# A gated-norm stage with its norm sums three products behind, its side sums dealt over the next group, and the next product's first weights made ahead

## The chip, the cores and the metric

The kernel runs on one core of a Trainium2 chip. The metric is the device time of one execution in microseconds. An execution is one launch of the whole program. The engines are named as in the profile: PE is TensorE (matmuls), PEld its weight loads, DVE VectorE, ACT ScalarE, POOL GpSimd, and SP SyncE, which here only issues DMAs.

## The reference

The program is one inference step of a small decoder trunk: a Mamba-2 (SSD) layer, then a sliding-window attention layer, each with an MLP. The part that the change touches is the end of the SSD mixer: the gate, a norm over each of eight groups of 256 features, and the output projection.

```python
def gated_group_rmsnorm(y, z, w):
    g = (y * jax.nn.silu(z)).astype(jnp.float32)
    shp = g.shape
    g = g.reshape(shp[:-1] + (N_GROUPS, shp[-1] // N_GROUPS))
    g = g * lax.rsqrt(jnp.mean(g * g, axis=-1, keepdims=True) + EPS)
    return (g.reshape(shp) * w.astype(jnp.float32)).astype(y.dtype)

# in mamba_mixer: z is the first D_INNER columns of rmsnorm(h) @ w_in, y the scan's output
    out = gated_group_rmsnorm(y, z, gate_w) @ w_out
```

D_MODEL is 1024, D_INNER 2048, N_GROUPS 8; there are 1104 columns (tokens): 1024 of the new sequence, 64 of the samples and 16 meta tokens.

## The kernel before

Activations lie with features on the 128 partitions and tokens along the free axis; one tile row covers 1104 tokens. Matmuls in fp32 are made of three products of a high and a low part (`mm3`): high weights by high data, high by low, low by high (L204, L205, L206). So everything that goes into a matmul is first split: ACT casts the high part, DVE or POOL subtracts it for the low part.

**The gates.** `gates_out` runs over the eight groups g. A group has two tiles of 128 features (j = 0, 1) and three blocks of columns c (384, 384 and 336, the table `CH`), so six gate products of 24 matmuls each. For each product ACT takes the tanh (L762) and DVE makes (t + 1) * z (L763). When both products of a block are done, POOL multiplies them by y (L770), which SP loads from DRAM (L754), ACT squares (L771), DVE adds the two squares (L772), and ACT and DVE split that sum of squares into its high part (`msh`, L247) and low part (`msl`, L248). The sum over the features is then two matmuls with a matrix of ones, L259 on the high part and L262 on the low part.

**When the sum comes.** The sum is not issued at once. `gate_group` puts it on the list `due` with a count, and `tick`, called after each product, counts down and issues what has reached 0. With the count 2 a block's sum comes two products later. What is issued is `gate_norm`: the two matmuls, then ACT copies the result to SBUF (L795). After the third block of a group it goes on at once: Ln and Exp on ACT (L798, L799), each of which loads its table, two scalings on DVE (L802, 128 x 1104 each, one for each j), and for the groups 0 to 5 the side sums.

**The side sums.** The output projection uses a scheme with seven products in place of eight on blocks of a two-by-two split; `side_sums` makes its sums of data. It takes the four halves r[0] to r[3] of the scaled tiles (two tiles, each in two halves of 552 columns), writes three of them and four sums of them to the DRAM buffer z_d (L818), and uses the norm's own tile gm for two of the sums (m and u). The last sum, r[2] - u, is made in two halves of 276 columns in small tiles o5 and written from there (L832). Groups 6 and 7 write their scaled tiles to DRAM (g_d) instead.

**Buffers.** y lives in two tiles that the groups take in turn, so group g + 2 is loaded into the tile of group g. The o5 tiles come from a ring of five (n1) which the high and low parts of the sums share; the n3 tiles of the products, from a ring of two. The sums have one PSUM bank.

**The output product.** `block_products` comes right behind the gates. `down_weights` is a generator that loads two tiles of weights and yields seven weight parts, some of them sums of weights on DVE (L1166, L1172), each split by ACT (L1047) and POOL (L1048). Its data come back from z_d (L1224) and are split by ACT and DVE (L1229, L1230). Its first outputs are added by DVE at L1264. At its sixth weight part `more` issues what is still on `due`, in a PSUM bank of the output product.

**What sets the order.** The code is written in one order, but a scheduler decides in what order each engine gets its instructions, from its own estimate of when each is ready. Within one engine the queue runs in order. Sums of groups above 0 are kept in program order on PE (`pin`).

## Time and profile before

| | us |
|---|---|
| three runs, median (lowest to highest) | 2924.53 (2918.5 to 2924.64) |
| the profiled execution | 2923.57 |
| its span in the profile | 2921.9 |
| gates, from the start of group 0's last norm sum to group 7's middle norm sum | 672.40 to 862.28 |
| first quarter of the output product's first block | 862.28 to 890.24 |
| DVE busy, whole span | 1895.0 |
| ACT busy, whole span | 1413.9 |
| POOL busy, whole span | 1386.1 |

In the rows of the profile the first number is a start or a stretch in us from the start of the span, "gm<-ms" reads output from input, and square brackets hold how long the engine had been idle before the instruction, and which instruction on another engine let it go. In a window's row each engine has its busy time and, in brackets, its number of instructions; the granted clock of PE, the DMA share and the rate in GB/s stand at the end.

### The profile page before, as it was taken

What the parts mean: (1) busy time and instruction counts of PE and PEld (TensorE: products, weight loads), DVE (VectorE), ACT (ScalarE), POOL (GpSimd) and SP (SyncE); (2) the same over time, 40 slices, a digit from 0 to 9 for tenths busy, and PEclk for the clock granted to TensorE, in tenths of its full rate; (3) what the DMA queues carried; (4) which work ended last, traced back from release to release, by engine and by line L of the source; (5) the groups of instructions that cost most, each with busy time, mean ns of one, the idle gap of its engine ahead of it and who ended that gap; (6) DMA issues with size and microseconds to landing.
All of it is one profiled execution on the core that took longest, in us unless ns stands there. A gap on an engine that the chain in (4) does not pass through costs nothing.

```text
span 2921.9 us, 51729 instructions
## 1 busy us (share of the span) xinstructions
PE 2816.2 (96%) x19895; PEld 2711.0 (93%) x19895; DVE 1895.0 (65%) x2995; ACT 1413.9 (48%) x2742; POOL 1386.1 (47%) x1279
## 2 busy tenths in 40 slices
PE   8999999988989999999999999999999999999998
PEld 6999999978889999999999999988889999999998
DVE  6788777765657675455466765666678454356675
ACT  6555555544555264444343325655555444433333
POOL 5566666665546615444266573312112444345562
PEclk9999999999999999999999999999999999999998
DMA  3344544447655224444554422447453444533422
GB/s 137 91 128 124 125 128 123 123 123 258 218 206 171 80 85 149 136 156 139 224 212 171 161 89 94 160 153 261 164 187 133 150 140 150 206 138 124 151 96 73
DMA packets 219470, 433.43 MB, mean 148 GB/s; under 512 B 30728, under 2 KB 128392, under 8 KB 216648
## 3 DMA queue, kind: packets, MB, share of 16 engines
q1 hardware_dynamic: 219224, 430.14, 44.3%
q8 instruction: 156, 2.56, 0.4%
q14 instruction: 90, 0.74, 0.1%
HBM read 302.71 MB, written 128.32 MB: 148 GB/s over the span
## 4 chain that ended last, share of the span: by engine, by line
PE 77%; DVE 10%; ACT 4%; issue 3%; DMA 3%; POOL 3%; SPq 0%; DVEq 0%; ACTq 0%; POOLq 0%
PE g L204 10%; PE g L206 10%; PE g L205 10%; PE mc L204 4%; PE mc L206 3%; PE mc L205 3%; PE ma L204 3%; PE ma L205 3%; PE ma L206 3%; PE md L206 3%; PE md L205 3%; PE md L204 3%; PE mb L206 3%; PE mb L204 3%; PE mb L205 3%
## 5 line engine op out<-in xcount | busy, mean ns | idle before, releaser
L1048 POOL TENSOR_TENSOR w<-s,w 128x384 fp32r<-128x384 f32 (+1 forms) x272 | 370.4, 1368 | 386.9 <-ACT w L1047 354.4
L206 PE MATMUL g<-S,w 128*128 128x384 f32 (+2 forms) x1584 | 531.1, 336 | 3.9 <-POOL w L171 3.3
L204 PE MATMUL g<-S,w 128*128 128x384 f32 (+2 forms) x1584 | 533.4, 337 | 1.3 <-DVE qp L1462 0.6
L205 PE MATMUL g<-S,w 128*128 128x384 f32 (+2 forms) x1584 | 533.6, 337 | 0.0
L1048 POOL TENSOR_TENSOR w<-raw,w 128x384 fp32r<-128x384 f32 (+1 forms) x204 | 264.3, 1301 | 286.2 <-ACT w L1047 255.2
L171 POOL TENSOR_TENSOR w<-raw,w 128x1024 fp32r<-128x1024 f32 x96 | 247.1, 2574 | 253.3 <-ACT w L170 189.3
L206 PEld LDWEIGHTS g<-S,w 128*128 128x128 f32 x1584 | 301.9, 191 | 5.8 <-POOL w L171 3.6
L204 PEld LDWEIGHTS g<-S,w 128*128 128x128 f32 x1584 | 301.3, 190 | 4.7 <-issue 1.5
L205 PEld LDWEIGHTS g<-S,w 128*128 128x128 f32 x1584 | 301.7, 190 | 0.9 <-issue 0.3
L1047 ACT CAST w<-s 128x384 fp32r<-128x384 f32 (+1 forms) x272 | 149.8, 557 | 313.0 <-DVE s L1172 84.7
L204 PE MATMUL ma<-S,w 128*128 128x276 f32 (+1 forms) x808 | 235.2, 291 | 8.0 <-DVE us L1264 6.7
L206 PE MATMUL ma<-S,w 128*128 128x276 f32 (+1 forms) x808 | 234.7, 290 | 0.0
L205 PE MATMUL ma<-S,w 128*128 128x276 f32 (+1 forms) x808 | 234.3, 290 | 0.0
L1047 ACT CAST w<-raw 128x384 fp32r<-128x384 f32 (+1 forms) x204 | 111.8, 555 | 154.6 <-PE mc L206 45.2
L602 DVE SCALAR_TENSOR_TENSOR fm<-xp,cv,fm 128x1024 f32<-128x1024 f32 x96 | 162.8, 1698 | 33.1 <-ACT fm L583 32.5
L204 PEld LDWEIGHTS ma<-S,w 128*128 128x128 f32 x808 | 153.3, 190 | 9.3 <-ACT S L1229 2.7
L205 PE MATMUL g<-R,w 128*128 128x384 f32 (+2 forms) x480 | 158.6, 330 | 0.0
L204 PE MATMUL g<-R,w 128*128 128x384 f32 (+2 forms) x480 | 158.1, 329 | 0.0
L206 PE MATMUL g<-R,w 128*128 128x384 f32 (+2 forms) x480 | 158.1, 329 | 0.0
L205 PEld LDWEIGHTS ma<-S,w 128*128 128x128 f32 x808 | 153.5, 190 | 0.0
L206 PEld LDWEIGHTS ma<-S,w 128*128 128x128 f32 x808 | 153.2, 190 | 0.0
L170 ACT CAST w<-raw 128x1024 fp32r<-128x1024 f32 x96 | 100.5, 1047 | 105.8 <-DMA raw<-in_w_o_dram 19.9
(492 smaller groups left out, 8696.0 us busy)
## 6 DMA issues: line engine op xcount, KB each, us to landing
raw<-in_w_up_dram SPq DMA_DIRECT2D x64, 512.0 KB
raw<-in_w_in_dram SPq DMA_DIRECT2D x48, 512.0 KB
raw<-in_w_downs_dram SPq DMA_DIRECT2D x64, 384.0 KB
w<-ws_o SPq DMA_DIRECT2D x48, 512.0 KB
w<-ws_q SPq DMA_DIRECT2D x40, 512.0 KB
ab<-acs_d SPq DMA_DIRECT2D x64, 256.0 KB
S<-t_d SPq DMA_DIRECT2D x18, 828.0 KB
S<-t_e SPq DMA_DIRECT2D x18, 816.0 KB
```

The lines of the kernel that those rows point to most:

```text
L170: nc.scalar.copy(out=wh, in_=raw)
L171: nc.gpsimd.tensor_tensor(out=wl, in0=raw, in1=wh.bitcast(F32), op=ALU.subtract)
L204: mm(out=out, lhsT=wh, rhs=xh, start=(first and k == 0), stop=False)
L205: mm(out=out, lhsT=wh, rhs=xl, start=False, stop=False)
L206: mm(out=out, lhsT=wl, rhs=xh, start=False, stop=(k == n - 1))
L602: nc.vector.scalar_tensor_tensor(out=acc[:, :SEQ], in0=xp[:, k:k + SEQ], scalar=cv[:, j, k:k + 1], in1=acc[:, :SEQ], op0=ALU.mult, op1=ALU ...
L1047: nc.scalar.copy(out=t[:, 0], in_=src)
L1048: nc.gpsimd.tensor_tensor(out=t[:, 1], in0=src, in1=t[:, 0].bitcast(F32), op=ALU.subtract)
```

## The change

The count in `due` goes from 2 to 3, so each norm sum comes three products behind its block. The work behind the third sum is no longer one piece: the first tile is scaled at once; the second scaling and the first part of the side sums are put at the head of `due` with the count 1, the rest with the count 2. For that `side_sums` becomes a generator with one yield; its other caller runs it through with `list`. With `own` it makes the last side sum as one operation of 552 columns in r[0], that is in the tile of y itself, and writes it from there. For the last group, at the fourth of its six steps, the generator of the output product's first weights is started and two of its parts are made; after the gates one pending sum (group 7's middle block) is issued in a bank of the output product, four more parts are made, and `block_products` takes these first.

```diff
--- before.py
+++ after.py
@@ -1,5 +1,6 @@
 from contextlib import ExitStack
 from functools import partial
+from itertools import chain
 
 import concourse.bass as bass
 import concourse.tile as tile
@@ -772,10 +773,10 @@
             nc.vector.tensor_tensor(out=g2[:, 0], in0=g2[:, 0], in1=g2[:, 1], op=ALU.add)
             self.tick()
             parts = self.sum_parts(g2[:, 0], n)
-            self.due.append([2, partial(self.gate_norm, g, c, y, parts, tmp)])
+            self.due.append([3, partial(self.gate_norm, g, c, y, parts, tmp)])
             if g == 0 and c < 2:
 
-                self.tick(2)
+                self.tick(3)
             yield
 
     def tick(self, n=1):
@@ -797,18 +798,24 @@
             return
         nc.scalar.activation(out=rs, in_=rs, func=AF.Ln, bias=self.eps4, scale=D / 256)
         nc.scalar.activation(out=rs, in_=rs, func=AF.Exp, scale=-0.5)
-        for j in range(2):
+
+        def scale(j):
             ft = 2 * g + j
             nc.vector.scalar_tensor_tensor(out=y[j], in0=y[j], scalar=self.nv[:, ft % 8, 6 + ft // 8:7 + ft // 8],
                                            in1=rs, op0=ALU.mult, op1=ALU.mult)
+        scale(0)
         if g < 2 * KB:
-            self.side_sums([t[:, i * T // 2:(i + 1) * T // 2] for t in y for i in range(2)],
-                           self.rz[g // KB][:, :, :, g % KB], rs[:, :T // 2], rs[:, T // 2:])
+
+            sums = self.side_sums([t[:, i * T // 2:(i + 1) * T // 2] for t in y for i in range(2)],
+                                  self.rz[g // KB][:, :, :, g % KB], rs[:, :T // 2], rs[:, T // 2:], True)
+            self.due[:0] = [[1, lambda: (scale(1), next(sums))], [2, lambda: list(sums)]]
         else:
+            scale(1)
             for j in range(2):
                 nc.sync.dma_start(out=self.gd[g][:, j], in_=y[j])
 
-    def side_sums(self, r, d, m, u):
+    def side_sums(self, r, d, m, u, own=False):
+
 
         nc = self.nc
         n = r[0].shape[1]
@@ -823,8 +830,14 @@
         to(0, 1, m)
         sub(r[1], r[3], r[1])
         to(1, 0, r[1])
+        yield
         sub(u, r[3], m)
         to(1, 1, u)
+        if own:
+
+            sub(r[0], r[2], u)
+            to(2, 1, r[0])
+            return
         for k in range(2):
             t = self.n1("o5")[:, :qw]
             cs = slice(k * qw, k * qw + qw)
@@ -854,8 +867,10 @@
         slots = [[[(t[:, 0], t[:, 1])] for t in ts] for ts in ([A5] + B + S[:4], [S[4], A5, A5] + S[:4])]
         load, parts = self.side_io(self.rz, slots)
         for g in range(1, G):
-            for _ in gate if g == 1 else self.gate_of(g, xs, yps):
-                pass
+            for k, _ in enumerate(gate if g == 1 else self.gate_of(g, xs, yps)):
+                if (g, k) == (G - 1, 3):
+                    gen = self.down_weights(self.i["w_outs"][0], 0)
+                    ahead = gen, [next(gen) for _ in range(2)]
             if g < G - 1:
                 self.split_ahead()
             if g == 4:
@@ -870,16 +885,19 @@
         cb.close()
         us = self.pool("us", ctx=co).tile([P, 4, nn], F32, name="us")
 
+        def free_bank_sums(n):
+
+            self.pstat = (self.pq, self.CHAIN[0][3], 1, 1024)
+            self.tick(n)
+            self.pstat = None
+
         def more(b, p, i):
             if (b, p) != (0, 0):
                 return
             if 1 <= i <= 4:
                 parts(0, i + 2)
             if i == 5:
-
-                self.pstat = (self.pq, self.CHAIN[0][3], 1, 1024)
-                self.tick(9)
-                self.pstat = None
+                free_bank_sums(9)
             if i == 6:
 
                 t = ya.tile([P, 4, nn], F32R, tag="y", bufs=1, name="A6")
@@ -887,8 +905,10 @@
                 slots[1][1] = [(rest, t[:, 0:2]), (t[:, 2:3], t[:, 3:4])]
         self.pq = self.pool("pq", space=PSUM, ctx=co)
         rd = [self.gd.get(g) for g in range(G)]
+        free_bank_sums(1)
+        ahead[1].extend(next(ahead[0]) for _ in range(4))
         self.block_products(self.i["w_outs"], big, us, slots, load, parts, [(0, 3, 4, 5, 6)], [(3, 6, 7, 8, 10)],
-                            (lambda: self.block_load(rd, 3, R0), lambda j: self.block_parts(j, R0)), more, (1, 1))
+                            (lambda: self.block_load(rd, 3, R0), lambda j: self.block_parts(j, R0)), more, (1, 1), ahead)
 
     def out_last(self, hts, done, norm):
 
@@ -1112,7 +1132,7 @@
         if not 2 <= f < 14:
             nc.sync.dma_start(out=rd[f].rearrange("p f (i n) -> p (f i) n", i=2), in_=r)
             return
-        self.side_sums([r[:, e] for e in range(4)], rt[(f - 2) // KB][:, :, :, (f - 2) % KB], m1, u)
+        list(self.side_sums([r[:, e] for e in range(4)], rt[(f - 2) // KB][:, :, :, (f - 2) % KB], m1, u))
 
     def up(self, layer, rd, rt, R0):
 
@@ -1230,7 +1250,9 @@
                 nc.vector.tensor_tensor(out=lo, in0=lo.bitcast(F32), in1=hi.bitcast(F32), op=ALU.subtract)
         return load, parts
 
-    def block_products(self, w, big, us, slots, load, parts, free, make, last, more, early=(0, 0)):
+    def block_products(self, w, big, us, slots, load, parts, free, make, last, more, early=(0, 0),
+                       ahead=None):
+
 
 
         nc = self.nc
@@ -1267,7 +1289,10 @@
                 banks = {}
                 hv = [[h[j][i][:, p] for i in range(2)] for j in range(2)]
                 uv = us[:, p]
-                for i, (wh, wl) in enumerate(self.down_weights(w[b], p)):
+                weights = self.down_weights(w[b], p)
+                if (b, p) == (0, 0) and ahead:
+                    weights = chain(ahead[1], ahead[0])
+                for i, (wh, wl) in enumerate(weights):
                     e = self.CHAIN[p % 2][i]
                     new = e not in banks
                     if new:
```

The line numbers of the changed kernel are higher by one to twenty-two: L802 is L804 there, L817 is L824, L818 is L825, L763 and L772 are L764 and L773, L248 is L249, L795 is L796, L754 is L755, L1166 is L1186, L1230 is L1250. Tiles carry a running number, which differs between the two.

On DVE, at the change from group 4 to group 5, before (gy_8540 is group 4's y, gm_8702 its norm, msl_8891 the low part of group 5's first sum):

```order
L802 SCALAR_TENSOR_TENSOR gy_8540<-gy_8540,nv_71,gm_8702 128x1104 x2
L763 SCALAR_TENSOR_TENSOR n3_8894<-n3_8894,g_8895 128x384
L817 TENSOR_TENSOR gm_8702<-gy_8540 128x552
L763 SCALAR_TENSOR_TENSOR n3_8894<-n3_8894,g_8922 128x384
L817 TENSOR_TENSOR gy_8540<-gy_8540 128x552
L817 TENSOR_TENSOR gm_8702<-gy_8540,gm_8702 128x552
L817 TENSOR_TENSOR o5_8884<-gy_8540,gm_8702 128x276
L817 TENSOR_TENSOR o5_8887<-gy_8540,gm_8702 128x276
L772 TENSOR_TENSOR n3_8894<-n3_8894 128x384
L248 TENSOR_TENSOR msl_8891<-n3_8807,msh_8890 128x384
```

The same place in the changed kernel (gy_8524 is group 4's y, gm_8718 its norm, msl_8852 and msl_8931 the low parts of group 5's first and middle sum):

```order
L773 TENSOR_TENSOR n3_8855<-n3_8855 128x384
L249 TENSOR_TENSOR msl_8852<-n3_8787,msh_8851 128x384
L804 SCALAR_TENSOR_TENSOR gy_8524<-gy_8524,nv_71,gm_8718 128x1104 x2
L249 TENSOR_TENSOR msl_8931<-n3_8855,msh_8930 128x384
L764 SCALAR_TENSOR_TENSOR n3_8934<-n3_8934,g_8935 128x336
L824 TENSOR_TENSOR gm_8718<-gy_8524 128x552
L764 SCALAR_TENSOR_TENSOR n3_8934<-n3_8934,g_8971 128x336
L824 TENSOR_TENSOR gy_8524<-gy_8524 128x552
L824 TENSOR_TENSOR gm_8718<-gy_8524,gm_8718 128x552
L824 TENSOR_TENSOR gy_8524<-gy_8524,gm_8718 128x552
```

The low part of group 5's first sum moved from behind all of group 4's scalings and side sums to ahead of both scalings; the scalings still stand together.

On ACT, around the copy of group 4's third sum, before (gy_8792 is group 5's y):

```order
L795 COPY gm_8702<-ms_8771 128x384
L170 CAST w_9046<-raw_9044 128x1024
L762 ACTIVATE n3_8807<-g_8835 128x384
L795 COPY gm_8702<-ms_8867 128x336
L798 ACT_TABLE_LOAD
L798 ACTIVATE gm_8702<-gm_8702,eps_67 128x1104
L771 ACTIVATE n3_8807<-gy_8792 128x384
```

and in the changed kernel (gy_8772 is group 5's y):

```order
L796 COPY gm_8718<-ms_8815 128x384
L772 ACTIVATE n3_8787<-gy_8772 128x384
L763 ACTIVATE n3_8855<-g_8890 128x384
L772 ACTIVATE n3_8855<-gy_8772 128x384
L772 ACTIVATE n3_8787<-gy_8772 128x384
L796 COPY gm_8718<-ms_8883 128x336
L799 ACT_TABLE_LOAD
```

The copy that starts group 4's norm, which stood between a product's tanh and its Ln, now has three squares of group 5 between it and the copy of the middle block.

On DVE, at the start of the output product, before (n3_9454 and msl_9519 belong to group 7's last block, S_90 is data of the output product, the s tiles are sums of weights):

```order
L772 TENSOR_TENSOR n3_9454<-n3_9454 128x336
L1230 TENSOR_TENSOR S_90<-S_90 128x1656
L248 TENSOR_TENSOR msl_9519<-n3_9454,msh_9518 128x336
L1166 TENSOR_TENSOR s_9564<-raw_9539 128x384
L1166 TENSOR_TENSOR s_9591<-raw_9537,raw_9539 128x384
```

and in the changed kernel, right behind group 6's two scalings (n3_9351 and msl_9422 belong to group 7's middle block, n3_9437 and msl_9503 to its last, hh is the output product's result):

```order
L773 TENSOR_TENSOR n3_9351<-n3_9351 128x384
L764 SCALAR_TENSOR_TENSOR n3_9437<-n3_9437,g_9438 128x336
L249 TENSOR_TENSOR msl_9422<-n3_9351,msh_9421 128x384
L1186 TENSOR_TENSOR s_9432<-raw_9427 128x384
L764 SCALAR_TENSOR_TENSOR n3_9437<-n3_9437,g_9470 128x336
L1192 TENSOR_TENSOR s_9432<-s_9432,raw_9425 128x384
L1250 TENSOR_TENSOR S_90<-S_90 128x1656
L773 TENSOR_TENSOR n3_9437<-n3_9437 128x336
L1286 TENSOR_TENSOR hh_7939<-md_9560,hh_7939 128x552
L1250 TENSOR_TENSOR S_90<-S_90 128x1656
L249 TENSOR_TENSOR msl_9503<-n3_9437,msh_9502 128x336
L1186 TENSOR_TENSOR s_9525<-raw_9425,raw_9427 128x384
```

The first sum of weights moved ahead of group 7's last products; the sum for the third part (s_9525 now, s_9591 before) moved behind two data parts (L1250) where it stood behind one.

## The prediction

> **What bounds the kernel now.** I read the busy times first, then the chain that ended last, then TensorE's waits in the stage that the change touches.
>
> ```profile
> span 2921.9 us, 51729 instructions
> PE 2816.2 (96%) x19895; PEld 2711.0 (93%) x19895; DVE 1895.0 (65%) x2995; ACT 1413.9 (48%) x2742; POOL 1386.1 (47%) x1279
> ...
> PE 77%; DVE 10%; ACT 4%; issue 3%; DMA 3%; POOL 3%; SPq 0%; DVEq 0%; ACTq 0%; POOLq 0%
> ```
>
> TensorE (PE) is busy 96% of the span. So the change can only win where TensorE stands still or runs at a lower clock. The waits of TensorE between 600 and 920 us, and a window (span, then busy time of PE, PEld, DVE, ACT, POOL, then granted clock, DMA share, GB/s) for the gates, for one undisturbed group of them, for the start of the output product, and for a stretch of output product at full rate:
>
> ```profile
> PE ms L262 <- DVE msl L248: 15.0, 5, 5.3
> PE md L204 <- ACT w L1047: 6.2, 1, 6.2
> ...
> 672.40:862.28 189.88, 171.66 (x975) 168.38 (x975) 113.74 (x127) 106.49 (x167) 97.37 (x62) 0.96 0.60 213
> 837.40:862.20 24.80, 24.80 (x147) 24.80 (x148) 10.68 (x16) 13.91 (x26) 9.93 (x9) 1.00 0.33 117
> 862.28:890.24 27.96, 20.02 (x133) 19.25 (x131) 22.46 (x21) 15.58 (x23) 17.87 (x12) 0.82 0.53 207
> 920.00:940.00 20.00, 20.00 (x160) 20.00 (x159) 12.23 (x13) 11.80 (x16) 10.11 (x8) 1.00 0.72 254
> ```
>
> The second window gives full rate in the gates: 24.80 / 147 = 0.1687 us a matmul, 24.8 us a group. At that rate the 975 matmuls of the first window take 164.5 us; it takes 189.88. So **25.4 us** are lost there: 18.2 us idle (189.88 − 171.66), the rest matmuls at a lower clock. The output product at full rate takes 20 / 160 = 0.125 us a matmul, so its start should take 133 × 0.125 = 16.6 us and takes 27.96: **11.3 us** lost. The change can take hold of these 36.7 us. The idle time is nearly all the low part of a norm sum that VectorE (DVE) makes late:
>
> ```profile
> 718.33 0.69 PE L262 MATMUL ms<-msl,ones_r 128*128 128x384 f32 x1 [5.26 <-DVE msl L248]
> 748.60 0.44 PE L262 MATMUL ms<-msl,ones_r 128*128 128x384 f32 x1 [4.39 <-DVE msl L248]
> 781.79 0.45 PE L262 MATMUL ms<-msl,ones_r 128*128 128x384 f32 x1 [2.79 <-DVE msl L248]
> ```
> ```profile
> 736.36 2.65 DVE L802 SCALAR_TENSOR_TENSOR gy<-gy,nv,gm 128x1104 f32<-128x1104 f32 x2 [0.98 <-ACT gm L799]
> 738.92 0.55 DVE L763 SCALAR_TENSOR_TENSOR n<-n,g 128x384 f32<-128x384 f32 x1
> 739.39 0.73 DVE L817 TENSOR_TENSOR gm<-gy 128x552 f32<-128x552 f32 x1
> 740.15 1.43 DVE L817 TENSOR_TENSOR gy<-gy 128x552 f32<-128x552 f32 x1
> 741.51 2.44 DVE L817 TENSOR_TENSOR gm<-gy,gm 128x552 f32<-128x552 f32 x1
> 743.88 0.54 DVE L763 SCALAR_TENSOR_TENSOR n<-n,g 128x384 f32<-128x384 f32 x1
> 744.34 1.59 DVE L817 TENSOR_TENSOR o<-gy,gm 128x276 f32<-128x276 f32 x2
> 745.85 2.69 DVE L248 TENSOR_TENSOR msl<-n,msh 128x384 fp32r<-128x384 f32 x1
> ```
>
> DVE does the scalings and side sums of one group in one lump (736.36 to 745.9), then the low part (745.85 + 2.69 = 748.54), and TensorE goes on at 748.60.
>
> **The change part by part.** *Three products behind.* A sum comes one product later on TensorE, 24 × 0.1687 = 4.0 us: about as long as the waits above. In the order of the changed kernel the low part of the next group's first sum stands ahead of both scalings and all side sums, so the lump no longer delays it. As far as the changed third sum of group 3, 475 matmuls after 672.40, the kernel before takes:
>
> ```profile
> 672.40:768.90 96.50, 84.67 (x475) 83.39 (x475) 62.27 (x63) 56.54 (x85) 53.17 (x32) 0.95 0.69 250
> 780.00:800.00 20.00, 18.21 (x96) 18.21 (x97) 7.37 (x13) 13.27 (x21) 10.51 (x7) 0.91 0.65 217
> ```
>
> At full rate 475 matmuls take 80.1 us. I leave 2.5 us for a wait at group 1's middle sum: it keeps its place on TensorE (3 matmuls later), but its low part now stands on DVE behind group 0's whole lump, which starts one product later. The bounds are 0 and the longest such wait, 5.26 us; I take about the middle. With 1.4 us for a lower clock after it: 84.0 us. **Term 1: 12.5 us gained.** On the clock: the slice with the 2.79 us wait has a granted clock of 0.91 over 20 us, 1.8 us' worth. The Trainium skill ("TensorE: Matmul & The Clock Gate", HAM oscillation) says that the rate is halved after an idle gap of about 3.4 us or more. By that the 2.5 us wait would cost no clock and the gain would be 13.9 us; the 2.79 us row, where the clock fell all the same, speaks against it.
>
> *What is late next.* The copy of a group's third sum (ACT L795, now L796) stood ahead of the next group's squares. It now stands behind three squares of the next group, which need that group's y. And y of group g+2 goes into the tile of group g, so its load (L754) must wait until the last side sum of group g is written out of that tile: the last write now comes from y itself (r[0]), where it came from o5 tiles. This closes a loop, one round a group: copy, Ln and Exp with their table loads, scalings, side sums, write, load, POOL product, square, copy. Its pieces:
>
> ```profile
> 729.48 0.44 ACT L795 COPY gm<-ms 128x336 f32<-128x336 f32 x1
> 730.88 1.28 ACT L798 ACT_TABLE_LOAD   x1
> 741.03 0.52 ACT L771 ACTIVATE n<-gy 128x384 f32<-128x384 f32 x1 [2.79 <-POOL gy L770]
> ```
> ```profile
> 837.07 0.83 SPq L754 DMA_DIRECT2D gy<-y_d  x2
> ```
> ```profile
> 838.40:842.00 3.60, 3.60 (x22) 3.60 (x21) 2.03 (x3) 1.09 (x3) 3.60 (x4) 1.00 0.94 346
> 842.00:846.00 4.00, 4.00 (x25) 4.00 (x24) 1.48 (x3) 1.72 (x4) 1.29 (x2) 1.00 0.14 56
> ```
> ```profile
> gy<-y_d SPq DMA_DIRECT2D x14, 552.0 KB
> z_d<-gy SPq DMA_DIRECT2D x24, 276.0 KB
> ```
> ```profile
> 845.34 1.00 POOL L770 TENSOR_TENSOR gy<-n,gy 128x384 f32<-128x384 f32 x1 [2.71 <-issue]
> ```
> ```profile
> 869.71 0.50 DVE L248 TENSOR_TENSOR msl<-n,msh 128x336 fp32r<-128x336 f32 x1
> ...
> L817 DVE TENSOR_TENSOR gm<-gy x6: 722/726/2822, 681.9 to 832.2; 128x552 f32<-128x552 f32 x6
> L817 DVE TENSOR_TENSOR gm<-gy,gm x6: 1518/1993/2925, 684.0 to 834.0; 128x552 f32<-128x552 f32 x6
> ```
>
> From the copy at 729.48 to the scaling at 736.36: 6.9 us. Scalings 2.65. Then on DVE the low part of the next sum 0.5, two gate products 1.1, and four sums: 0.73 + 1.43 + 2.44 + 1.59 = 6.2 as they stood (the last as the two halves took), or 0.72 + 0.72 + 1.52 + 0.72 = 3.7 at the shortest of their groups (lowest/median/highest in ns). The trace doesn't show when a write to z_d is finished. It is bounded below by 276 KB at 346 GB/s, 0.8 us, and above by a whole y load, 4.9 us (issue at 837.07; the DMA rate falls from 346 to 56 GB/s at 842.0). I take 2.5: the y load's 1,104 KB at 346 GB/s are 3.2 us, so 1.7 us are fixed, plus 0.8. With 0.3 for its issue: 2.8. The y load 4.9. Three POOL products at 1.0 and a square 0.5: 3.5. Sum: 26.0 us with the short sums, 28.5 with the long; I take the middle, **27.3 us**. The Trainium skill ("DMA: Bandwidth & Descriptors", Anatomy of one DMA) gives about 2.0 us fixed for a DMA; with 0.8 for the bytes that makes 2.8 where I take 2.5, and the round 27.6. No row here shows the end of a write.
>
> A group of products needs 24.8 us, so the loop, not TensorE, sets the pace from group 3 on. Counted from group 3's third sum, with two casts of the output product's data (1.57 each, 866.30 below) ahead of the first round's copy, the copies of groups 4, 5 and 6 come at 27.3 + 3.1 = 30.4, 57.7 and 85.0 us. On DVE both scalings of group 6 stand ahead of the low part of group 7's middle sum: 85.0 + 6.9 + 2.65 + 1.5 (square sum, high and low part at 0.5) = **96.0 us**, where the kernel before has this sum 862.28 − 768.90 = 93.4 us after the same point. **Term 2: 2.6 us lost**, where TensorE alone, with 500 matmuls at 0.1687 = 84.4 us, could have gained 9.0.
>
> *Weights made ahead.* At the output product's start TensorE waits for the first weights:
>
> ```profile
> 871.27 0.60 PE L204 MATMUL md<-R,w 128*128 128x276 f32 x1 [6.19 <-ACT w L1047]
> 873.85 0.60 PE L206 MATMUL md<-R,w 128*128 128x276 f32 x1 [1.75 <-POOL w L1048]
> ```
> ```profile
> 867.91 1.88 DVE L1230 TENSOR_TENSOR S<-S 128x1656 fp32r<-128x1656 f32 x1 [2.03 <-ACT S L1229]
> 870.13 1.02 DVE L1166 TENSOR_TENSOR s<-raw 128x384 f32<-128x384 f32 x2
> ...
> 873.83 1.35 DVE L1172 TENSOR_TENSOR s<-s,raw 128x384 f32<-128x384 f32 x1 [0.89 <-POOL w L1048]
> ```
> ```profile
> 866.30 1.57 ACT L1229 CAST S<-S 128x1656 fp32r<-128x1656 f32 x1 [0.96 <-DMA S<-z_d]
> ```
>
> Two of seven parts are now made before, so the 6.19 + 1.75 us go. The third part's sum (s_9525) stands on DVE behind, from the middle sum's low part on: 1.02 + 0.5 + 1.35 + 1.88 + 0.5 + 0.7 (the copy-add L1286, taken as a 552-wide add) + 1.88 + 0.5, then its own 1.02, a cast of 0.5 on ACT and 1.0 on POOL: 10.9 us. TensorE has two parts' products for it, 2 × 19 × 0.125 = 4.8 us, so it waits some 6 us. With 16.6 us of matmuls and 2 us of lower clock: 24.6 us against 27.96. **Term 3: 3.4 us gained.** The last stretch from group 3's third sum then takes 96.0 + 24.6 = 120.6 us; before, 121.3. That gains 0.7 us. But the late copies also mean waits of TensorE on the way, the longest, some 6 us, at group 7's middle sum, and waits bring a lower clock as in the slice above; I take 2.2 us for it, so terms 2 and 3 together come to **−1.5 us**.
>
> *The single last side sum* takes 6 DVE operations and 6 DMAs of SP's queue away; both are beside TensorE's work, and count only in the loop, above. The y of group g+2 is the one load that SP's queue holds back behind these writes; behind it stand weight loads for products one and two groups on, which have their slack in the ring of raw tiles.
>
> **Sum.** 12.5 − 1.5 = 11 us against the profiled execution's 2923.57 us: 2912.6. That execution lies 0.96 us below the median of the three runs, 2924.53; I say **2913 us**.
>
> **The rivals.** *The dealing hides everything.* If y comes in time (a write that ends in 0.8 us and short sums make the loop 26.0 − 1.7 = 24.3 us, under the 24.8 of TensorE), terms 2 and 3 gain 9 + 3.4 with term 1's 12.5, less 2 for what remains: 18 to 25 us, about 2901. For it: the medians of the sums are the short ones. Against it: the copy's place behind the squares is fixed.
>
> *The loop is a little longer*, 30 to 31 us: three further rounds at 3 us each eat term 1 almost whole, 12.5 − 9 = 2 to 5 us left, about 2920. For it: the sums that took 2.44 where 1.52 is their shortest, and DMAs at a share of 0.94 beside them.
>
> *Slower.* From a loop of 31.5 us on, the four rounds lose more than 12.5 + 3.4. At 33 us (a write that takes the whole 4.9, long sums, a y load stretched by 2 us by weight loads beside it) it is four times 5.7 = 22.8 lost against 15.9 gained: 7 us slower, about 2931. It is one mechanism: y waits for the last write from its own tile. Against it: the bounds must fall together.
>
> *The change doesn't act.* The queues are ordered by a scheduler from its own estimates; if the sums find their low parts as late as now (the lump's pieces dealt but all ahead of it), the time stays, 2922 to 2925. Against it: the order shows the low part ahead of the scalings for group 5.
>
> **How the numbers follow.** The forecast (6 to 17 us gained) 0.45, hidden wholly 0.17, a little longer loop 0.15, slower 0.13, no effect 0.10. About 0.2% (5.8 us) is what a measurement of this kernel tells from no change: faster 0.45 + 0.17 = 0.62, same 0.15 + 0.10 = 0.25, slower 0.13. The range: 2898 leaves out the best of the first rival, 2931 most of the slower case, some 0.2 in all.
>
> **What would show it.** Right: no wait of TensorE on the low part (now L249) for groups 2 and 3, third sums of groups 4 to 6 some 27 us apart, the y load issued right behind the last write of z_d (L825) and late, the copy L796 behind squares, a wait of about 6 us at group 7's middle sum, and a wait of the third product chain for a weight cast at the output product's start. Wrong: a y load that is issued well before its first use, group spacing of 24.8 us (first rival), or of over 31 us (slower), or waits on L249 of 3 to 5 us in every group as before (no effect).

## The result and the profile after

The changed kernel takes 2937.63 us (median of 6 runs, 2932.37 to 2942.17), the kernel before beside it 2924.04 us: a ratio of 1.0047, 95% interval 1.0037 to 1.0057. It is 13.6 us slower; the forecast was 11 us faster. The profiled execution of the changed kernel took 2937.08 us.

The page after, its span, its busy times and the chain that ended last:

```profile
span 2935.4 us, 51695 instructions
...
PE 2821.2 (96%) x19895; PEld 2714.7 (92%) x19895; DVE 1896.2 (65%) x2989; ACT 1414.1 (48%) x2742; POOL 1382.3 (47%) x1279
...
PE 74%; DVE 8%; issue 5%; DMA 5%; POOL 4%; ACT 3%; SPq 0%; DVEq 0%; POOLq 0%; ACTq 0%
```

The work is the same (DVE has the six operations less). The waits in the gates and the output product's start tell what changed; the columns are total us, times, longest:

```profile
PE ms L260 <- ACT msh L248: 17.8, 6, 5.0
...
POOL gy L771 <- DMA gy<-y_d: 8.6, 3, 6.6
...
PE mc L205 <- ACT w L1067: 4.5, 1, 4.5
...
PE ms L260 <- ACT gm L796: 3.4, 3, 1.7
...
PE ms L263 <- DVE msl L249: 0.6, 1, 0.6
```

The wait on the low part that the prediction built on is gone: 15.0 us before, 0.6 now. TensorE waits 17.8 us on the *high* part instead (2.1 before), 3.4 us on the copy that empties the sums' one PSUM bank (1.1 before), and GpSimd waits 8.6 us for y (not at all before; all from 672 to 895 us of the span). The three stretches of the prediction's terms, cut at the same matmuls:

```profile
670.53:764.70 94.17, 85.35 (x476) 84.39 (x475) 58.84 (x58) 50.16 (x79) 49.20 (x29) 0.95 0.70 251
764.70:865.87 101.17, 88.03 (x503) 85.81 (x501) 53.87 (x64) 56.05 (x89) 49.11 (x33) 0.96 0.45 158
865.87:894.74 28.87, 22.45 (x131) 21.10 (x131) 23.21 (x22) 16.05 (x24) 17.00 (x12) 0.77 0.61 222
```

Before, they took 96.5, 93.4 and 27.96 us. So 2.3 us were gained in the first and 7.8 and 0.9 lost in the others: 6.4 us slower. The other 7 us lie outside: 9.0 us more behind 894.74, 1.9 less ahead of 670.53, in code that is the same but for a few rows. That share is taken up below.

Where the waits come from is read from timelines. Group 1's middle sum, the first long wait (PE, then DVE):

```profile
694.96 0.69 PE L260 MATMUL ms<-msh,ones_r 128*128 128x384 f32 x1 [4.23 <-ACT msh L248]
...
689.24 2.90 DVE L824 TENSOR_TENSOR gm<-gy,gm 128x552 f32<-128x552 f32 x1
692.06 0.49 DVE L764 SCALAR_TENSOR_TENSOR n<-n,g 128x336 f32<-128x336 f32 x1
692.48 0.72 DVE L824 TENSOR_TENSOR gy<-gy,gm 128x552 f32<-128x552 f32 x1
693.12 1.24 DVE L773 TENSOR_TENSOR n<-n 128x384 f32<-128x384 f32 x1
```

Now it is the square sum (L773), one step ahead of the high part, that stands behind group 0's side sums on DVE. A shorter wait, at group 2's middle sum, is for the copy that empties the bank:

```profile
726.76 0.45 PE L260 MATMUL ms<-msh,ones_r 128*128 128x384 f32 x1 [1.74 <-ACT gm L796]
```

Group 6's first sum (PE, then ACT):

```profile
835.22 0.69 PE L260 MATMUL ms<-msh,ones_r 128*128 128x384 f32 x1 [4.53 <-ACT msh L248]
...
832.35 1.28 ACT L800 ACT_TABLE_LOAD   x1
833.64 1.12 ACT L800 ACTIVATE gm<-gm 128x1104 f32<-128x1104 f32 x1
834.67 0.91 ACT L248 CAST msh<-n 128x384 fp32r<-128x384 f32 x2
```

Here the high parts stand behind the table load and the Exp of group 5's norm on ACT. And group 3's first sum (PE, SP, POOL):

```profile
746.68 0.69 PE L260 MATMUL ms<-msh,ones_r 128*128 128x384 f32 x1 [2.85 <-ACT msh L248]
...
721.51 0.32 SPq L825 DMA_DIRECT2D z_d<-gy  x1
725.97 2.79 SPq L176 DMA_DIRECT2D ws_q<-w  x2
728.82 0.42 SPq L167 DMA_DIRECT2D raw<-in_w_in_dram  x1
729.34 1.27 SPq L755 DMA_DIRECT2D gy<-y_d  x2
...
735.16 1.98 POOL L771 TENSOR_TENSOR gy<-n,gy 128x384 f32<-128x384 f32 x2 [1.22 <-issue]
```

Group 3's y is loaded 7.8 us after group 1's last side-sum write was issued; before the change that load was issued at 718.87, 1.0 us behind the last write. In SP's queue two writes of weights (ws_q) and a load stood ahead of it. The row of POOL names no releaser, but its queue stood at this product until the y load landed at 734.95. Each of the three waits comes from another place in an in-order queue.

### The profile page after: what moved, and what is told of

Read it like the earlier page. It is cut to its first block, busy times and chain, and to the rows that moved or that the text cites. A ratio compares the mean times of both kernels' runs of the same rounds, so it can differ in the third digit from the quotient of the medians.

```text
span 2935.4 us, 51695 instructions
## 1 busy us (share of the span) xinstructions
PE 2821.2 (96%) x19895; PEld 2714.7 (92%) x19895; DVE 1896.2 (65%) x2989; ACT 1414.1 (48%) x2742; POOL 1382.3 (47%) x1279
## 4 chain that ended last, share of the span: by engine, by line
PE 74%; DVE 8%; issue 5%; DMA 5%; POOL 4%; ACT 3%; SPq 0%; DVEq 0%; POOLq 0%; ACTq 0%
PE g L205 10%; PE g L206 10%; PE g L207 10%; PE mc L205 3%; PE mc L207 3%; PE mc L206 3%; PE ma L205 3%; PE ma L207 3%; PE ma L206 3%; PE md L206 2%; PE mb L207 2%; PE md L207 2%; PE mb L206 2%; PE mb L205 2%; PE md L205 2%
## 5 line engine op out<-in xcount | busy, mean ns | idle before, releaser
L205 PE MATMUL ma<-S,w 128*128 128x276 f32 (+1 forms) x808 | 236.0, 292 | 10.5 <-DVE us L1286 6.7
L205 PE MATMUL mc<-S,w 128*128 128x276 f32 (+1 forms) x512 | 148.6, 290 | 3.9 <-DVE hh L1286 2.2
```

What stands on the lines that cost most here:

```text
L205: mm(out=out, lhsT=wh, rhs=xh, start=(first and k == 0), stop=False)
```

## The experiments

Two measures go through all of them. The **stage** runs from the program's 4,290th to its 5,412th matmul (counted from 0), from group 0's last norm sum through the gates and the first quarter of the output product: 220.2 us before, 226.2 changed. The **round** is the mean distance from a group's first scaling to the next group's, groups 1 to 6. Both are of one profiled execution each; medians and ratios are of the timed runs, each beside the kernel before on the same chip. TensorE's waits at the norm sums, from 672 to 895 us, stand in the order low part / high part / copy; "y" is GpSimd's wait for y before its product (in E6 another 8.4 us, in E9 another 1.9, are put down to y before a weight's low part).

| kernel | median us | ratio to before, 95% interval | stage | round | low / high / copy | y |
|---|---|---|---|---|---|---|
| before | 2924.04 | | 220.2 | 29.3 | 15.0 / 2.1 / 1.1 | 0 |
| changed | 2937.63 | 1.0047 [1.0037, 1.0057] | 226.2 | 30.4 | 0.6 / 17.8 / 3.4 | 8.6 |
| E1 changed, o5 back | 2937.63 | 1.0051 [1.0037, 1.0066] | 231.6 | 31.6 | 1.5 / 13.2 / 9.1 | 7.6 |
| E2 changed, two behind | 2935.44 | 1.0040 [1.0026, 1.0054] | 228.2 | 31.4 | 1.4 / 1.9 / 17.9 | 4.8 |
| E3 changed, one lump | 2933.52 | 1.0039 [1.0024, 1.0054] | 226.8 | 30.4 | 1.0 / 19.0 / 4.0 | 5.8 |
| E4 changed, weights late | 2938.24 | 1.0054 [1.0039, 1.0069] | 231.3 | 30.8 | 0.6 / 20.4 / 2.2 | 14.3 |
| E5 before, own tile | 2933.19 | 1.0028 [1.0019, 1.0038] | 229.6 | 31.5 | 2.0 / 2.7 / 17.8 | 4.5 |
| E6 before, three behind | 2937.02 | 1.0039 [1.0025, 1.0054] | 231.5 | 31.0 | 1.7 / 14.9 / 8.8 | 6.1 |
| E7 before, dealt | 2928.38 | 1.0012 [1.0003, 1.0022] | 225.1 | 29.8 | 4.3 / 4.5 / 10.3 | 3.6 |
| E8 before, weights ahead | 2930.53 | 1.0019 [1.0010, 1.0028] | 223.3 | 29.8 | 14.7 / 3.1 / 1.1 | 0 |
| E9 before, sum in gm | 2934.11 | 1.0035 [1.0022, 1.0048] | 232.6 | 32.0 | 0 / 3.8 / 22.1 | 9.2 |
| E10 before, two banks | 2930.14 | 1.0020 [1.0009, 1.0031] | 223.6 | 29.1 | 12.6 / 5.1 / 0 | 5.2 |
| E11 E2 with two banks | 2925.49 | 1.0003 [0.9994, 1.0012] | 217.0 | 28.5 | 6.4 / 10.8 / 0 | 8.7 |
| E12 changed, two banks | 2929.97 | 1.0020 [1.0010, 1.0029] | 223.0 | 30.2 | 7.3 / 14.3 / 0 | 5.3 |
| E13 before, gm free | 2926.33 | 1.0008 [0.9999, 1.0018] | 222.6 | 29.3 | 4.5 / 13.6 / 0 | 6.7 |
| E14 changed, gm free | 2929.82 | 1.0020 [1.0010, 1.0030] | 224.8 | 29.9 | 6.2 / 13.5 / 1.2 | 9.0 |
| E15 E13 with two banks | 2926.22 | 1.0009 [0.9999, 1.0018] | 223.6 | 29.5 | 4.0 / 14.0 / 0 | 6.7 |
| E16 E11 with gm free | 2929.04 | 1.0014 [1.0005, 1.0023] | 223.2 | 29.7 | 5.6 / 15.0 / 0 | 16.0 |
| E17 before, no splits | 2917.95 | 0.9976 [0.9966, 0.9986] | 209.9 | 26.7 | 5.3 / 1.5 / 1.1 | 0 |
| E18 changed, no splits | 2932.25 | 1.0029 [1.0017, 1.0040] | 221.0 | 28.9 | 0.8 / 4.0 / 11.1 | 9.2 |

### E1 to E4: one part of the change undone

The first theory was the prediction's loop: the write out of y's own tile, the y load and the squares close a round that is longer than TensorE's 24.8 us.

E1 makes the last side sum in the o5 tiles again:

```diff
-                                  self.rz[g // KB][:, :, :, g % KB], rs[:, :T // 2], rs[:, T // 2:], True)
+                                  self.rz[g // KB][:, :, :, g % KB], rs[:, :T // 2], rs[:, T // 2:])
```

> The changed kernel, but the last side sum is made in the two o5 tiles again. Loop theory (each round from scaling to scaling runs through the last write out of y's own tile, the y load and the squares): the y load is issued within 1.5 us of the last side-sum write, where it comes 3.6 to 7.8 us behind it in the changed kernel; the mean from first scaling to y load falls from 16.5 to about 12.5 us, rounds of groups 1 to 5 from 30.6 to about 27 us, time 2922 to 2928 us. Order theory (the third sum's copy and the low parts are late by their places in the queues, y or not): rounds stay at 30 us or more, 2934 to 2940 us.

E2 puts the sums two products behind again:

```diff
-            self.due.append([3, partial(self.gate_norm, g, c, y, parts, tmp)])
+            self.due.append([2, partial(self.gate_norm, g, c, y, parts, tmp)])
...
-                self.tick(3)
+                self.tick(2)
```

> The changed kernel, but the norm sums come two products behind as before. Loop theory: the round loses one product, 4.0 us, so TensorE's pace of 24.8 us rules again in part: rounds of 26.5 to 27.5 us, time 2918 to 2926 us. Order theory (a sum two behind finds its low part behind the scalings and side sums): waits of TensorE on the low part of 3 to 5 us a group are back, 2932 to 2942 us.

E3 issues the scalings and side sums as one lump:

```diff
-            self.due[:0] = [[1, lambda: (scale(1), next(sums))], [2, lambda: list(sums)]]
+            scale(1)
+            list(sums)
```

> The changed kernel, but both scalings and all side sums are issued at once behind the third sum. Loop theory: the last side-sum write comes about 3 us sooner after the first scaling, so rounds of 27 to 28 us and 2924 to 2930 us. Order theory: the lump stands ahead of the low parts again, waits on them as before the change, 2936 to 2942 us.

E4 makes the weights in their own loop:

```diff
-                if (g, k) == (G - 1, 3):
-                    gen = self.down_weights(self.i["w_outs"][0], 0)
-                    ahead = gen, [next(gen) for _ in range(2)]
+                pass
...
-        ahead[1].extend(next(ahead[0]) for _ in range(4))
...
-                            ..., more, (1, 1), ahead)
+                            ..., more, (1, 1))
```

> The changed kernel, but the output product's first weights are made in its own loop (the sum of group 7's middle block is still issued in a bank of the output product). If the weights ahead gain what I took (3.4 us at the output product's start): 2940 to 2943 us, with the wait of 6 us for the first weight back and that of 4.65 us for the third one gone. If they cost (their DVE sums and casts stand ahead of group 7's own work): 2930 to 2935 us, and group 7's middle sum waits less than 5.1 us.

None gives the loss back: 2933.5 to 2938.2 us. E1 and E2 end where the order theory put them (E2 not for its reason: the low part's waits stay at 1.4 us), E3 and E4 between their two forecasts. The loop theory falls in its first form. In E1 the y load does come close behind the last o5 write (0.4 to 1.9 us in four of five rounds), but the o5 sums themselves come late, so the y load still lies 12 to 18 us after the scaling (15.8 in the mean, where 12.5 was expected). In E2 the changed kernel's 17.8 us on the high part fall to 1.9, and the copy's 3.4 us grow to 17.9. E4 speaks a little for the weights ahead, 0.6 us, which is within the uncertainty; in the profiled executions its stage is 5.1 us longer than the changed kernel's, and its part behind the stage 4.2 us shorter.

### E5 to E8: one part of the change alone

E5 adds to the kernel before only the own tile, E6 only the count 3 (with group 7's middle sum in a bank of the output product), E7 only the dealing, E8 only the weights ahead; the edits are the parts of the diff above.

> The kernel before, with one edit: the last side sum is one operation in y's own tile. Loop theory with what the first four runs showed (before the change y arrives some 15 us ahead of its first use): the y load comes 3 to 5 us later after the first scaling (13 to 15 us, 10.3 before), and the gates and the output product's first quarter take as long as before within 3 us (220.2 us). Queue theory for what is lost behind the gates (6 DMAs fewer put every later DMA on another of the queues that they take in turn): 4 to 9 us more than before behind that point, 2926 to 2933 us. Against it: nothing behind that point, 2921 to 2926 us.

> The kernel before, with one edit: sums three products behind (group 7's middle sum in a bank of the output product), the lump and the o5 tiles as before. Loop theory: the o5 tiles share a ring of five with the sums' parts, which are now held a product longer, so the side sums wait for TensorE's sums; y load 14 us or more after the first scaling, the stage 4 to 10 us longer than 220.2. If three behind does what it says: waits on the low part fall from 15 to under 5 us and the stage is 5 to 12 us shorter. Queue theory: as many DMAs as before, so nothing lost behind the stage (under 2.5 us).

> The kernel before, with one edit: the second scaling and the side sums dealt over the next two products. Loop theory: the last side-sum write comes later after the scaling by 2 to 5 us, but y has slack, so the stage stays within 3 us of 220.2. If dealing lets the low parts by: 4 to 8 us shorter. Behind the stage under 2.5 us lost by the queue theory. Total 2918 to 2927 us.

> The kernel before, with one edit: the output product's first weights made ahead. By the prediction's third term the output product's start is 3.4 us shorter: 2919 to 2922 us. By the run with late weights beside the changed kernel, which was slower by only 0.6 us: within 1.5 us of before. Behind the stage under 2.5 us lost.

Every part alone makes the kernel slower: by 7.6, 11.4, 2.7 and 4.9 us (medians beside before's 2925.64). They sum to 26.6 us, twice what they cost together. None of the four came as expected. E5's total lies 0.2 us above the 2926 to 2933 of the queue theory, with the time lost in the stage and not behind it; E6's stage is 11.3 us longer, where 4 to 10 were expected; E7 and E8, which might have gained, lie above their ranges. TensorE's and GpSimd's waits in E5:

```profile
PE ms L260 <- ACT gm L796: 17.8, 5, 4.4
...
POOL gy L771 <- DMA gy<-y_d: 4.5, 5, 1.9
...
PE ms L260 <- ACT msh L248: 2.7, 3, 1.3
...
PE ms L263 <- DVE msl L249: 2.0, 2, 1.2
```

E5 replaces two operations by one, which writes into y's own tile, and drops one of two writes. It removes the wait on the low part as thoroughly as the whole change does (15.0 to 2.0 us), since the scheduler now puts the low part ahead (that of group 2's first sum at 700.08, ahead of the scaling at 705.85; before, at 717.72, behind the scaling at 706.52 and all side sums); and 17.8 us of wait on the copy take its place. I had expected its stage within 3 us of before; it is 9.4 us longer. E8's weights are as the prediction's third term had them in kind: the first wait goes, and a wait of 7 us for the third part comes.

The queue theory for the loss behind the stage falls as well: E5 has six DMAs fewer, and its part behind the stage, up to the last matmul, is the shortest of all (2017.3 us, before 2020.0, changed 2029.5; 2017.6 to 2026.0 in the others up to E16). With one profiled execution of each kernel, this spread can be put down neither to the edits nor to chance; how much of the changed kernel's 9 us there belongs to the change stays open.

### E9 to E12: the norm's tile and the PSUM bank

The second theory: the next sum needs the one PSUM bank, the bank needs its copy, and the copy needs gm and a place in ACT's queue. E9 is E5 with the sum in gm, which holds gm longer and frees y's tile of the last write:

```diff
-            sub(r[0], r[2], u)
-            to(2, 1, r[0])
+            sub(m, r[2], u)
+            to(2, 1, m)
```

> The run with the one edit 'last side sum in y's own tile', but the sum goes into the norm's tile gm instead, so y waits for no write of the last sum. Y theory (the write out of y's tile delays y, and that costs the 7.5 us): GpSimd's waits for y fall from 4.5 us to under 1, y load 11 to 12 us after the first scaling, 2923 to 2928 us. Bank theory (the next group's first copy must wait until gm and its place in ACT's queue are free, the one PSUM bank of the sums stays full, and TensorE's next sum waits for the bank): gm is held even longer, TensorE's waits on the copy stay at 15 us or more, 2930 to 2938 us.

E10, E11 and E12 give the sums a second bank in place of one of the products' banks:

```diff
-                self.more_banks(cr, 4)
+                self.more_banks(cr, 3, 2)
```

> The kernel before, with two PSUM banks for the sums and one less for the products. Bank theory: TensorE waited only 1.1 us on the copy before the change, the low part's 15 us stay: within 3 us of before, 2921 to 2927 us.

> The changed kernel with sums two behind (2935.4 us, 17.9 us of waits on the copy), with two PSUM banks for the sums and one less for the products. Bank theory: those waits fall under 4 us and the time to 2920 to 2928 us. Other theory (the bank only shows where the same late work is met first: squares and high parts are late as well): waits on the high part take their place, 2932 to 2938 us.

> The changed kernel with two PSUM banks for the sums and one less for the products. Both theories: only 3.4 us of its waits are on the copy, 17.8 on the high part, so 2932 to 2939 us; under 2928 us would say that the bank was behind the late high parts too.

E9 goes as this theory said: 22.1 us on the copy, 2934.1 us. GpSimd's wait for y does not fall, though, with y's load issued 0.4 to 0.5 us behind the last write; it doubles to 9.2 us. The second bank takes the copy's wait away wherever it is put. E2 and E11, which differ in the bank alone:

```profile
PE ms L260 <- ACT gm L796: 17.9, 5, 4.4
```
```profile
PE ms L260 <- ACT msh L248: 10.8, 5, 3.8
...
PE ms L263 <- DVE msl L249: 6.4, 7, 1.5
```
```profile
671.80:900.00 228.20, 200.22 (x1124) 195.47 (x1123) 137.66 (x145) 125.17 (x193) 120.30 (x75) 0.93 0.57 202
```
```profile
672.90:889.80 216.90, 192.47 (x1123) 186.82 (x1122) 136.33 (x145) 125.77 (x196) 117.17 (x75) 0.97 0.60 213
```

E11's stage is 11.3 us shorter than E2's, with a granted clock of 0.97 for 0.93, and the ratio falls from 1.0040 to 1.0003: **shown**, the bank is one part of E2's loss. In the changed kernel it gives back more than was expected from 3.4 us of waits (1.0047 to 1.0020; E12 missed its expected range by 2 us), but of the 8.8 us between the profiled executions only 3.3 us lie in the stage; 6.4 us lie behind it, where the cause is open. The kernel before, which waited there for 1.1 us only, becomes slower with the same edit (1.0020, where none was expected). But the waits at the sums only come down from 21.2 to 17.2 us in E11, and not at all in E12 (21.8 and 21.6): they come back on the high and low parts, in smaller pieces. The stage of the changed kernel holds 30.7 us at half rate, that of E12 20.5: by my estimate some 5 us of matmuls, more than the whole 3.3.

### E13 to E16: gm freed at the scalings

If a closed round through gm set the pace, freeing gm early would shorten it. All four side sums are made in y's tile, in place:

```diff
+        if own:
+            sub(r[0], r[1], r[0])
+            to(0, 1, r[0])
+            sub(r[1], r[3], r[1])
+            to(1, 0, r[1])
+            yield
+            sub(r[3], r[3], r[0])
+            to(1, 1, r[3])
+            sub(r[2], r[2], r[3])
+            to(2, 1, r[2])
+            return
         sub(m, r[1], r[0])
         to(0, 1, m)
...
-        if own:
-
-            sub(r[0], r[2], u)
-            to(2, 1, r[0])
-            return
```

> The kernel before, but the four side sums are made in place in y's tile, so that the norm's tile gm is free once both scalings are done; y's next load then waits for all the writes. Norm-tile theory (a closed round: third copy, Ln and Exp, scalings, side sums through gm, first copy of the next group into gm, third copy): scaling to first copy falls from 12.7 to under 9 us, the round from 29.3 to 25 to 27 us, time 2910 to 2920 us. Y theory (what counts is when y's tile comes free): y load 3 to 6 us later, GpSimd waits for y, rounds of 30 us or more, 2926 to 2936 us.

> The changed kernel with the same edit. Norm-tile theory: scaling to first copy falls from 14.7 to under 10 us, round from 30.3 to under 28 us, 2916 to 2928 us. Y theory: y, already late in the changed kernel, comes later still: 2938 to 2950 us.

> The kernel before with side sums in place and two PSUM banks for the sums (one less for products). Norm-tile theory with the bank in the same round: as the run with side sums in place alone, or faster by up to 5 us; 2907 to 2919 us. Y theory: 2928 to 2938 us.

> The changed kernel with sums two behind, two banks and side sums in place. Against its twin with the side sums through gm (2925.5 us, round 28.5 us): norm-tile theory 2910 to 2920 us, round under 27 us; Y theory 2928 to 2938 us.

The leg from scaling to the next group's first copy does fall, in E13 from 12.7 to 5.1 us. The leg from first to third copy grows from 10.5 to 18.4 us, and the round is 29.3 us as before. The edit also holds y's tile longer: the y load comes 13.9 us after the scaling (10.3 before) and GpSimd waits 6.7 us for y. So freeing gm in this way does not shorten the round; whether gm closed it and y took its place is not shown. The time lies at the lower end of what the Y theory forecast, but its round of 30 us or more does not come. E14 and E15 end between the two forecasts, and E16 in the Y theory's. In the changed kernel freeing gm gives back as much as the second bank (1.0047 to 1.0020), again mostly behind the stage (1.4 us in it and 7.8 behind). Both together, in E16, are slower than the second bank alone (2929.04 and 2925.49 us).

### E17 and E18: the other work on the engines

What all kernels share in this stage are the splits of later weights (key, value and query), which run on GpSimd and ACT between the gates. Both kernels without them; they are then split where they are used, and only the stage is to be compared:

```diff
             if g < G - 1:
-                self.split_ahead()
+                self.ahead = self.ahead[1:]
```

> The kernel before, without the six splits of later weights (key, value and query) that are put into the gates; those weights are split where they are used, so only the gates stage is to be compared. Shared-engine theory (no single closed round: a block's square sum passes GpSimd, ACT and DVE in turn, in order, between the casts, products and copies of those splits, and each wait that goes is met again at the next): the stage falls from 220.2 us to 205 to 214, the round from 29.3 to under 27.5 us. If a closed dependency sets the round: within 3 us of 220.2.

> The changed kernel without those splits; stage against 226.2 us. Shared-engine theory: with the engines free, the change acts more as it was meant to, so the stage falls by more than the kernel before does, to 205 to 214 us, at or below the twin without the change. If a closed dependency sets the round: within 3 us of 226.2, and 4 us or more above the twin.

The stage of the kernel before, of the changed kernel, of E17 and of E18, then E17's waits and E18's:

```profile
673.43:893.66 220.23, 193.94 (x1124) 189.70 (x1124) 138.98 (x151) 124.63 (x192) 117.00 (x75) 0.95 0.58 209
671.60:897.80 226.20, 197.81 (x1123) 193.29 (x1122) 138.00 (x145) 124.81 (x193) 116.64 (x75) 0.93 0.57 202
```
```profile
671.30:881.20 209.90, 193.32 (x1124) 189.06 (x1123) 124.96 (x151) 121.65 (x189) 93.11 (x64) 0.95 0.50 180
671.10:892.00 220.90, 198.00 (x1123) 193.77 (x1122) 131.69 (x145) 120.70 (x189) 96.12 (x65) 0.94 0.49 171
```
```profile
PE ms L262 <- DVE msl L248: 5.3, 4, 1.9
...
PE ms L259 <- ACT msh L247: 1.5, 2, 0.8
...
PE ms L259 <- ACT gm L795: 1.1, 1, 1.1
```
```profile
PE ms L260 <- ACT gm L796: 11.1, 4, 4.5
POOL gy L771 <- DMA gy<-y_d: 9.2, 4, 5.4
...
PE ms L260 <- ACT msh L248: 4.0, 2, 3.4
```

For the kernel before, the shared-engine theory holds: stage 220.2 to 209.9 us, round 29.3 to 26.7, waits at the sums 18.2 to 7.9 us, with no dependency among the gates' own operations altered. The splits' DMAs go with them (DMA share 0.58 to 0.50), and E17 does not separate the two. Even with the splits done later it beats both kernels: 2917.95 us, 0.9976 [0.9966, 0.9986]. E18 goes against what I expected of the same theory. Its stage falls by only 5.2 us and is 11.1 us longer than its twin's. With the engines freer, waits that the change brings are left: 11.1 us of waits on the copy and 9.2 us of GpSimd for y, where the twin has 1.1 and none.

## Why the prediction was wrong

**What bounds the kernel: right as far as it went.** The low part behind the lump was TensorE's wait, and it went (15.0 to 0.6 us). What failed is the step from there to the time. "At full rate 475 matmuls take 80.1 us. I leave 2.5 us" took the wait for the cost. The low part was only the last of seven steps of a block (tanh, gate product, y product, square, square sum, high part, low part) on three engines that are shared; with it moved ahead, TensorE met the step before, or the bank, a little later: all its waits at the norm sums are 21.8 us, where they were 18.2. What the prediction named as signs did come in part: no wait on the low part for groups 2 and 3, the copy behind squares, a wait of 5.0 us at group 7's middle sum (for some 6), and one for the third weight part. The change acted as described, and that did not make the kernel faster.

Forecast and result are 24.6 us apart: 10.2 lie in term 1, 5.2 in term 2, 2.1 in term 3 with the 2.2 us allowed for waits beside it, and 7.1 outside the three stretches, which the prediction left out of its sum without a reason.

**Term 1, 12.5 us gained; measured 2.4** (96.6 to 94.2 us between the same two matmuls; 2.3 by the windows' edges). Of the 14.1 us above full rate, 8.8 are three waits (4.23, 1.74 and 2.85 us), and the granted clock of 0.95 over 94.17 us explains 4.7 more. The 4.23 us at group 1's middle sum lies within the bounds 0 and 5.26. The 1.74 us are the bank's copy, which the prediction never priced. The 2.85 us I had not looked for because I let the loop set the pace "from group 3 on": group 3's own y was already late, behind group 1's write.

**Term 2, 2.6 us lost; measured 7.8.** The third copies of groups 4, 5 and 6 came 31.0, 62.9 and 91.2 us after group 3's third sum, for 30.4, 57.7 and 85.0, and group 7's middle sum 101.2 us after it, for 96.0. From scaling to scaling the rounds from group 1 to group 6 were 30.0, 33.5, 28.4, 32.9 and 26.9 us, where I took 27.3. The last side-sum write is issued 9.5 to 13.6 us after the first scaling (9.2 in the prediction). From there the y load is issued 3.6 to 3.8 us later in three of five rounds and 5.3 in a fourth, each time as soon as that write has landed; in the fifth it is 7.8, with other transfers ahead in SP's queue. I took 2.8. In E5, where the load waits for the same write, it is 2.1 to 3.5. The Trainium skill ("DMA: Bandwidth & Descriptors", Anatomy of one DMA), with about 2.0 us fixed, would have made it 3.1. That figure is fitted there to DMAs that GpSimd issues, and these are issued by SP; the measurement decides.

**Term 3, 3.4 us gained; measured 0.9 lost.** The mechanism was right: the first weight waits go, and TensorE waits for the third part (4.5 us and 1.1, for "some 6 us"). The lower clock was mis-sized: 0.77 granted over 28.87 us is 6.6 us, where I took 2.

**On the clock.** In the changed kernel's trace the waits of 4.23, 2.85 and 4.53 us all lie at stretches of half rate, which are 3.41 or 6.83 us long; that of 1.74 us does not. The Trainium skill ("TensorE: Matmul & The Clock Gate", HAM oscillation) puts the bound at about 3.4 us; the 2.85 us wait here, like the 2.79 us before, speaks for a lower one. E17's wait of 1.85 us, from 713.90 to 715.75, is followed by half rate from 716.08. The length of a wait alone does not decide: in each of the twenty traces all stretches of half rate begin on one grid of 3.41 us steps, and a step at full rate with more than 1.89 us of idle TensorE is always followed by half rate. E17's wait falls wholly into one step (712.67 to 716.08); an edge at 725.27 cuts the 1.74 us wait in two. The grid starts anywhere from 0.09 to 3.33 us into the span (at 1.65 both before and in the changed kernel), so the same wait can bring half rate in one execution and none in another. Ahead of 600 us, in code that all the kernels share, twelve traces have a stretch of half rate and eight have none.

**The rivals.** The sign was that of *slower*, but not its mechanism: the mean round, 30.4 us, stayed below the 31.5 us from which it was to decide (two single rounds were longer), and keeping y's load from waiting for that write (E1, E9) gave nothing back, though E9 holds gm longer at the same time. *The loop is a little longer*, 30 to 31 us, met the round, 30.4, but at 2920 us: it spent term 1's gain, which was not there. The error in both is the same: a wait removed was booked as a gain, and the path that runs just behind it was priced by the hops that I could name.

**What is shown and what is open.** Shown: the low part's wait is replaced and not removed; each part alone costs time; on the changed kernel a second bank or an early gm gives back some 8 of 13.6 us, of which 3.3 and 1.4 us lie in the stage, and neither helps the kernel before; 10.3 us of the stage of the kernel before go when the splits go. Not shown: which of y and the copy costs the rest in the changed kernel, and how much of the 9 us behind the stage is the change's. A third y tile would have told the first; it was not tried.

## What to carry to other kernels

Where a block passes several in-order engines on its way to TensorE, the last releaser of a wait is not its price: work out when the *second* latest would have let go (the step before, the bank, the next load), and book only the difference. If a stage's pace does not change when a tile or a wait is freed, try next what it does without the other work on its engines: here that gave 10.3 us, where no reordering of the kernel before gave any. A cheap trial that undoes the change part by part would have told more than the trace: here each part, alone, already had the wrong sign.

## What the runs showed that was not expected

VectorE's work in the stage became shorter when *GpSimd's* went. The same 151 operations took 138.98 us in the kernel before and 124.96 in E17, with 11 GpSimd operations fewer (75 to 64); two operations of one shape there differ widely (a low part of 128x384 took 2.69 us at 745.85 before, beside a GpSimd subtraction, and 0.56 at 860.47). The lengthening goes with the overlap: in the kernel before, the ten 128x384 adds (L772) of the stage that no GpSimd operation overlaps took 0.55 to 0.56 us, the four others 1.86 in the mean and up to 2.79. The gate products (L763), which read PSUM, took 0.54 to 0.56 us with and without. So the splits cost DVE some 14 us besides their own time.

Replacing two 276-wide subtractions by one 552-wide one in y's own tile, with one write for two, cost 7.6 us of 2925 (E5). Other work took other places in the queues then, and the next y load waited for that write; the run does not tell how much each cost.

One of E14's ten executions took 5466.37 us; no other run of any kernel did, and nothing in the runs explains it.
